# Differential attention: the causal mask added on VectorE with the maximum, instead of by matrix products on TensorE

## The chip, the cores and the metric

The kernel runs on one core of a Trainium2 chip. The core has TensorE for matrix products (PE in the profile; PEld is its loading of weights), VectorE (DVE), ScalarE (ACT), GpSimd (POOL), and SyncE (SP), which here issues DMAs. They work side by side and wait for each other by semaphores. SBUF is the working memory of 128 partitions; PSUM, in eight banks, takes the results of TensorE. The metric is the time of one execution on the device in microseconds (us).

## What is computed

A decoder trunk of two layers over 512 tokens of 1024 numbers. Each layer is a feed-forward block, a token mixer, cross-attention into 256 memory tokens, and another feed-forward block, each followed by a LayerNorm. The mixer of the first layer is differential attention with 8 heads; only it is touched. Cut to what matters:

```python
def diff_attention(x, w_qkv, w_o, lam_q, lam_k, subln_g, cos, sin, lam_init):
    ...
    q = rope(q, c5, s5)
    k = rope(k, c5, s5)
    lam = jnp.exp(jnp.sum(lq[0] * lk[0])) - jnp.exp(jnp.sum(lq[1] * lk[1])) + lam_init
    ...
    def block(args):
        qblk, i = args
        s = jnp.einsum('bqhcd,bkhcd->bhcqk', qblk, k).astype(jnp.float32) * scale
        qpos = i * DA_QBLOCK + jnp.arange(DA_QBLOCK)
        mask = kpos[None, :] <= qpos[:, None]
        s = jnp.where(mask, s, jnp.finfo(jnp.float32).min)
        p = jax.nn.softmax(s, axis=-1)
        a = p[:, :, 0] - lam * p[:, :, 1]
        return jnp.einsum('bhqk,bkhe->bqhe', a.astype(v.dtype), v)
    ...
    o = o * lax.rsqrt(jnp.mean(jnp.square(o), axis=-1, keepdims=True) + LN_EPS)
```

Each head has two score maps (m = 0 and 1), each with its own softmax, and the second is subtracted from the first with a factor. A query sees only keys that do not come after it.

## The kernel before

**Precision.** Every float32 operand of a large product is split into a high part, made by ScalarE, and a low rest, made by VectorE (`split`, lines 114 and 115). A product is then three products: high by high, low by high, high by low (lines 201 to 203). So VectorE and ScalarE must work for each weight before TensorE can use it.

**The stage.** `diff_attention` weaves two streams of work. The main stream (`da_main`) projects values, queries and keys head by head, and at the end multiplies by the first half of the output matrix. After each projection come the rotary step (`da_rope`, lines 941 to 944) and the splits into `qk` and `low` tiles (954 to 970). The side stream (`da_side`) runs over 32 steps, one for each head h and query block i of 128 tokens. In step s it makes the scores of step s (`da_scores`), turns the probabilities of step s - 2 (`da_turn`, four transposes at most, line 479), and multiplies those of step s - 3 with the values (`da_out`, lines 1014 and 1015). After the last block of a head come the norm's factor on GpSimd (1030 to 1033), the scaling on ScalarE (1039) and a last transpose (`da_turn_out`). `weave` gives the side stream a turn for each 900 ns of main work by a fixed table of costs (`W_SC` and others), so where the side stream's work stands among the projections does not hang on what an instruction really takes. Each engine's queue is then put in order when the program is built, and each engine works through its own queue in that order.

**The scores (`da_scores`).** Query block i sees n = 128, 256, 384 or 512 keys. For each map, two products of n columns make the scores in a PSUM bank (lines 983 and 984). A third product, identity by mask in bfloat16, adds a large negative number above the diagonal in the last 128 columns (985). VectorE reduces each row to its negated maximum `mx` (988). ScalarE takes the exponential of PSUM minus the maximum, writes the probabilities `p` to SBUF, and sums each row with a second instruction, the read of its accumulator (both line 989). VectorE then forms the factor from the two sums (992, 993) and subtracts the second map from the first (994). The scores, the transposes and the output products share six PSUM banks in turn (`aux`). There are four `p` tiles; each step takes two.

**Constants.** `da_constants`, beside the first feed-forward block, loads the mask into a temporary tile and casts mask and identity to bfloat16 (1501 to 1504). `NEG`, the number above the diagonal, is minus two to the power of 100.

Of the kernel before, what the change touches and what calls it, by code (L numbers as in the profile page):

```python
# [12 lines left out]
AF = mybir.ActivationFunctionType  # L13
ALU = mybir.AluOpType
AX = mybir.AxisListType
PSUM = bass.MemoryType.PSUM

P = 128
D = 1024
S = 512  # L20
# [13 lines left out]
NEG = -float(2.0**100)  # L34
# [65 lines left out]
def drain(units):  # L100
    for _ in units:
        pass


class Trunk:
# [76 lines left out]
    def mm(self, name):  # L182
        return self.mmp.tile([P, S], F32, tag="mm", name=name)
# [789 lines left out]
    def da_scores(self, st, i):  # L973

        nc = self.nc
        q, k, n = st["q"], st["k"], (i + 1) * P
        qi, kn = slice(i * P, n), slice(0, n)
        mx, rc, cf = self.small("mx"), self.small("rc", (P, 1)), self.small("cf", (P, 1))
        sm = st["sm"][:, i]
        sc = [self.aux("sc")[:, :n] for m in range(2)]  # L980
        mm = nc.tensor.matmul
        for m in range(2):
            mm(sc[m], q[m][:, qi], k[0][m][:, kn], start=True, stop=False)
            mm(sc[m], q[m][:, qi], k[1][m][:, kn], start=False, stop=False)
            mm(sc[m][:, n - P :], self.identr, self.maskr, start=False, stop=True)
        p = [self.tmp("p")[:, :n] for m in range(2)]
        for m in range(2):
            nc.vector.tensor_reduce(mx[:, m : m + 1], sc[m], AX.X, ALU.max, negate=True)
            nc.scalar.activation(
                p[m], sc[m], AF.Exp, bias=mx[:, m : m + 1], accum_out=sm[:, m : m + 1]  # L990
            )
        nc.vector.reciprocal(rc, sm[:, 1:2])
        nc.vector.scalar_tensor_tensor(cf, sm[:, 0:1], self.nlam, rc, ALU.mult, ALU.mult)
        nc.vector.scalar_tensor_tensor(p[0], p[1], cf, p[0], ALU.mult, ALU.add)
        st["p", i] = p[0]
# [73 lines left out]
    def da_side(self):  # L1069

        n = DA_H * NT
        for s in range(n + LS + 2):
            h, i = divmod(s, NT)
            if s < n:
                while h >= len(self.heads) or self.clock < self.heads[h][0] + LEAD:
                    yield WAIT
                self.da_scores(self.heads[h][1], i)
                yield W_SC[i]
            h, i = divmod(s - LT, NT)
            if 0 <= s - LT < n:  # L1080
                self.da_turn(self.heads[h][1], i)
                yield W_T[i]
            h, i = divmod(s - LO, NT)
            if 0 <= s - LO < n:
                while len(self.heads[h][1]["v"]) < NT:
                    yield WAIT
                self.da_out(self.heads[h][1], i)
                yield W_O[i]
            h, i = divmod(s - LS, NT)
            if 0 <= s - LS < n and i == NT - 1:  # L1090
                self.da_scale(self.heads[h][1])
                yield W_E[0]
            h, i = divmod(s - LS - 1, NT)
            if 0 <= s - LS - 1 < n and i == NT - 1:
                self.oT[h] = self.da_turn_out(self.heads[h][1])
                yield W_E[1]
# [370 lines left out]

    def mixer(self, layer, ln):
        if layer == 0:
            bufs = dict(low=4, rt=2, a=4, p=4, o=1, qk=8, _x=0, v=4, oT=11)  # L1470
            with self.other_pools(), self.phase_pool(("v", "v"), "rt", **bufs):
                self.diff_attention(layer, ln)
            self.close_side()
        else:
            w = self.a["xa_wkv"][layer]
            self.later = ExitStack()
            self.later.enter_context(self.late_pools())
            self.kvp = self.later.enter_context(self.pool("kv"))
            with self.phase_pool(("pooled", "pooled"), "sq", pooled=20, sq=1):
                with self.tc.high_priority():  # L1480
                    keys = self.load_cols(w, 0, "rawe")
                    self.load_memory()
                    ahead = [self.halves(t, "we", "we") for t in keys]
                    self.pool_weights()
                    self.raw_order = ["rawe", "raw", "raw"]
                side = self.pool_mixer(layer, ln)
                next(side)
                self.kv = []
                self.weave(self.first_heads(layer, ahead), side, 900, 6000)
                drain(self.early_kv(layer, (1,), self.ahead))  # L1490
            self.close_side()

    def da_constants(self):
        nc, a = self.nc, self.a
        c = lambda shape, name, dt=F32: self.ropep.tile(shape, dt, name=name)
        self.rope = c([P, 2], "rope")
        nc.sync.dma_start(self.rope, a["rope"])
        self.ropeC, self.ropeS = c([P, S], "ropeC"), c([P, S], "ropeS")
        self.rope_tables()
        m = self.tmp("sp", (P, P))  # L1500
        nc.sync.dma_start(m, a["mask"])
        self.maskr, self.identr = (c([P, P], n, mybir.dt.bfloat16) for n in ("maskr", "identr"))
        nc.vector.tensor_copy(self.maskr, m)
        nc.vector.tensor_copy(self.identr, self.ident)
        self.subg = c([P, 1], "subg")
        nc.sync.dma_start(self.subg, a["da_subln_g"].rearrange("a p -> p a"))
        nc.vector.tensor_scalar(self.subg, self.subg, 1.0 - LAM_INIT, None, ALU.mult)
# [29 lines left out]
```

## Time and profile before

| | us |
|---|---|
| median of 3 runs | 1947.85 |
| lowest and highest | 1946.04, 1948.92 |
| the profiled execution | 1946.09 |
| its span, first to last instruction | 1944.3 |
| busy: TensorE, VectorE, ScalarE, GpSimd | 1913.8, 1560.1, 1012.3, 334.3 |

The granted clock of TensorE is 0.998 in the mean. A group of instructions is shown by line, engine, operation, "out<-in" by the program's tile names with the shapes, then busy us and the mean ns of one, then the engine's idle time just before them with what ended it. In the chain of work, each piece is what the following one waited for, or the instruction before it on its engine.

### The profile page before, as it was taken

The numbers are of one execution on the slowest core, as the hardware profiler recorded it, in microseconds if no ns is written. First come the engines' busy times: TensorE is split into PE (matmuls) and PEld (weight loads), VectorE is DVE, ScalarE is ACT, GpSimd is POOL, SyncE is SP. The second block draws the span as 40 slices with busy tenths as digits, with TensorE's granted clock in tenths as the row PEclk, the third lists the DMA queues.
The fourth block names the chain that finished last, engine by engine and source line by source line (L and its number), as shares of the span: only waits on it lengthen the run. The fifth ranks groups of instructions, "written<-read, shape, count | busy, mean of one in ns | idle before, by whom it ended". The sixth has DMA issues, their size and how long they took to land.

```text
span 1944.3 us, 32440 instructions
## 1 busy us (share of the span) xinstructions
PE 1913.8 (98%) x13052; PEld 1741.6 (90%) x13052; DVE 1560.1 (80%) x2200; ACT 1012.3 (52%) x1537; POOL 334.3 (17%) x317
## 2 busy tenths in 40 slices
PE   9999999999999999999999999999999999999998
PEld 8999998888778888999998999999898889999996
DVE  7988987888867557798888888988886468888886
ACT  6555553566655444655554555555455436555552
POOL 3212121111211002312110322122110013111211
PEclk9999999999999999999999999999999999999999
DMA  9878772322135425977695598778445336777861
GB/s 255 198 169 181 169 154 66 90 66 88 44 109 174 128 68 132 226 167 147 153 202 140 105 217 174 169 155 175 142 141 152 109 87 115 192 175 170 183 143 44
DMA packets 254182, 280.58 MB, mean 144 GB/s; under 512 B 9168, under 2 KB 221648, under 8 KB 254032
## 3 DMA queue, kind: packets, MB, share of 16 engines
q0 software_dynamic: 95808, 102.77, 32.4%
q1 hardware_dynamic: 158224, 175.74, 28.2%
q8 instruction: 102, 1.67, 0.3%
q14 instruction: 48, 0.39, 0.1%
HBM read 274.28 MB, written 4.20 MB: 143 GB/s over the span
## 4 chain that ended last, share of the span: by engine, by line
PE 72%; DVE 16%; DMA 4%; ACT 4%; issue 2%; POOL 1%; SPq 0%; DVEq 0%; POOLq 0%; ACTq 0%
PE x L202 6%; PE x L201 6%; PE x L203 6%; PE z L202 4%; PE z L201 4%; PE z L203 4%; DVE wl L115 4%; PE ps L203 3%; PE ps L202 3%; PE ps L201 3%; DMA ra<-in_ffn_w_in_dram 3%; PE px L201 2%; PE px L203 2%; PE px L202 2%; PE xq L202 2%
## 5 line engine op out<-in xcount | busy, mean ns | idle before, releaser
L636 POOL DMA_DIRECT2D ra<-in_ffn_w_in_dram x132 | 170.4, 1313 | 989.1 <-DVE wl L115 968.8
L114 ACT CAST wh<-ra 128x1024 fp32r<-128x1024 f32 x184 | 193.3, 1052 | 212.6 <-PE x L202 59.0
L115 DVE TENSOR_TENSOR wl<-ra,wh 128x1024 fp32r<-128x1024 f32 x184 | 223.7, 1221 | 68.8 <-ACT wh L114 68.0
L114 ACT CAST wh<-rc 128x1024 fp32r<-128x1024 f32 x136 | 142.8, 1053 | 120.7 <-PE x L202 43.6
L201 PE MATMUL x<-xh,wh 128*128 128x256 f32 x704 | 196.8, 280 | 1.3 <-ACT xh L114 1.3
L203 PE MATMUL x<-xh,wl 128*128 128x256 f32 x704 | 196.4, 279 | 0.6 <-DVE wl L115 0.6
L202 PE MATMUL x<-xl,wh 128*128 128x256 f32 x704 | 196.4, 279 | 0.1
L201 PE MATMUL x<-xe,wh 128*128 128x256 f32 x704 | 195.6, 278 | 0.0
L202 PE MATMUL x<-xe,wh 128*128 128x256 f32 x704 | 195.5, 278 | 0.0
L203 PE MATMUL x<-xe,wl 128*128 128x256 f32 x704 | 195.4, 278 | 0.0
L114 ACT CAST wh<-b 128x1024 fp32r<-128x1024 f32 x112 | 117.8, 1051 | 131.0 <-PE x L202 63.2
L115 DVE TENSOR_TENSOR wl<-rc,wh 128x1024 fp32r<-128x1024 f32 x136 | 164.5, 1220 | 22.9 <-ACT wh L114 22.9
L115 DVE TENSOR_TENSOR wl<-b,wh 128x1024 fp32r<-128x1024 f32 x112 | 136.8, 1221 | 41.3 <-ACT wh L114 41.3
L201 PEld LDWEIGHTS x<-xh,wh 128*128 128x128 f32 x704 | 133.1, 189 | 2.8 <-ACT xh L114 1.5
L202 PEld LDWEIGHTS x<-xl,wh 128*128 128x128 f32 x704 | 133.4, 190 | 1.9 <-DVE xl L115 0.6
L203 PEld LDWEIGHTS x<-xh,wl 128*128 128x128 f32 x704 | 133.1, 189 | 0.8 <-DVE wl L115 0.8
L201 PEld LDWEIGHTS x<-xe,wh 128*128 128x128 f32 x704 | 132.6, 188 | 1.3
L202 PEld LDWEIGHTS x<-xe,wh 128*128 128x128 f32 x704 | 132.5, 188 | 1.4
L203 PEld LDWEIGHTS x<-xe,wl 128*128 128x128 f32 x704 | 132.4, 188 | 0.0
L203 PE MATMUL y<-xh,wl 128*128 128x256 f32 x352 | 98.9, 281 | 3.4 <-DVE wl L115 2.3
L201 PE MATMUL y<-xh,wh 128*128 128x256 f32 x352 | 98.2, 279 | 0.4 <-ACT wh L114 0.4
L202 PE MATMUL z<-xe,wh 128*128 128x256 f32 x352 | 97.8, 278 | 0.3 <-DVE xe L115 0.3
(404 smaller groups left out, 6075.8 us busy)
## 6 DMA issues: line engine op xcount, KB each, us to landing
ra<-in_ffn_w_in_dram POOLq DMA_DIRECT2D x132, 512.0 KB, 7.0
rc<-in_ffn_w_in_dram SPq DMA_DIRECT2D x88, 512.0 KB, 6.3
b<-in_ffn_w_out_dram SPq DMA_DIRECT2D x60, 512.0 KB, 5.0
ra<-in_ffn_w_in_dram SPq DMA_DIRECT2D x44, 512.0 KB, 5.0
rc<-in_ffn_w_in_dram POOLq DMA_DIRECT2D x44, 512.0 KB, 7.7
b<-in_ffn_w_out_dram POOLq DMA_DIRECT2D x16, 512.0 KB, 12.4
raw<-in_da_w_qkv_dram SPq DMA_DIRECT2D x16, 512.0 KB, 5.2
raw<-in_xa_wkv_dram SPq DMA_DIRECT2D x8, 1024.0 KB, 5.5
```

The source lines that it names most:

```text
L114: self.nc.scalar.copy(hi, src),
L115: self.nc.vector.tensor_sub(lo, src, hi.bitcast(F32)),
L201: mm(out, w[0], x[0], start=start, stop=False, skip_group_check=again)
L202: mm(out, w[0], x[1], start=False, stop=False, skip_group_check=again)
L203: self.last_mm = mm(out, w[1], x[0], start=False, stop=stop, skip_group_check=again)
L636: self.last_more = nc.gpsimd.dma_start(t, source(*block), accum_op=ALU.add)
```

## The change

The third product of each map goes, and with it the bfloat16 tiles and their casts. In its place stands a float32 tile of 128 by 512: 384 columns of zeros, set by GpSimd, and the mask in the last 128 columns, loaded by SyncE's queue. Taken from column 512 - n on, its n columns are zero but for the last 128. One VectorE instruction, `tensor_tensor_reduce`, adds this to the scores in PSUM, multiplies by -1, writes the n results to the `p` tile in SBUF, and keeps the least of each row, starting from two to the power of 100: that is the negated maximum, as before. The exponential then reads `p` with a factor of -1 and writes `p` in place. The phase's pools get one buffer more (`mask=1`).

```diff
             mm(sc[m], q[m][:, qi], k[0][m][:, kn], start=True, stop=False)
-            mm(sc[m], q[m][:, qi], k[1][m][:, kn], start=False, stop=False)
-            mm(sc[m][:, n - P :], self.identr, self.maskr, start=False, stop=True)
-        p = [self.tmp("p")[:, :n] for m in range(2)]
+            mm(sc[m], q[m][:, qi], k[1][m][:, kn], start=False, stop=True)
+        p, mask = [self.tmp("p")[:, :n] for m in range(2)], self.mask[:, S - n :]
         for m in range(2):
-            nc.vector.tensor_reduce(mx[:, m : m + 1], sc[m], AX.X, ALU.max, negate=True)
+            top = mx[:, m : m + 1]
+            nc.vector.tensor_tensor_reduce(p[m], sc[m], mask, -1.0, -NEG, ALU.add, ALU.min, top)
             nc.scalar.activation(
-                p[m], sc[m], AF.Exp, bias=mx[:, m : m + 1], accum_out=sm[:, m : m + 1]
+                p[m], p[m], AF.Exp, bias=top, scale=-1.0, accum_out=sm[:, m : m + 1]
             )
...
         n = DA_H * NT
+        self.mask = self.tmp("mask")
+        self.nc.gpsimd.memset(self.mask[:, : S - P], 0.0)
+        self.nc.sync.dma_start(self.mask[:, S - P :], self.a["mask"])
         for s in range(n + LS + 2):
...
-            bufs = dict(low=4, rt=2, a=4, p=4, o=1, qk=8, _x=0, v=4, oT=11)
+            bufs = dict(low=4, rt=2, a=4, p=4, o=1, qk=8, _x=0, v=4, oT=11, mask=1)
...
-        m = self.tmp("sp", (P, P))
-        nc.sync.dma_start(m, a["mask"])
-        self.maskr, self.identr = (c([P, P], n, mybir.dt.bfloat16) for n in ("maskr", "identr"))
-        nc.vector.tensor_copy(self.maskr, m)
-        nc.vector.tensor_copy(self.identr, self.ident)
```

## The prediction

> **What bounds the kernel now.** I first read the span in slices (TensorE's granted clock is full throughout), then looked for the stage that the change touches. The masked scores run from about 376 to 576 us, so I asked for the busy time of each engine in four stretches of it. Columns: stretch, its length, then busy us (and count) of PE, PEld, DVE, ACT, POOL, clock, DMA share, GB/s.
>
> ```profile
> 376.00:409.00 33.00, 33.00 (x223) 29.12 (x222) 29.17 (x65) 21.23 (x57) 3.31 (x4) 1.00 0.22 65
> 409.00:455.00 46.00, 46.00 (x294) 39.87 (x293) 39.56 (x84) 31.62 (x83) 8.48 (x12) 1.00 0.25 69
> 455.00:528.00 73.00, 69.27 (x387) 55.44 (x386) 63.10 (x131) 48.99 (x128) 16.67 (x20) 1.00 0.18 58
> 528.00:576.00 48.00, 46.90 (x281) 38.93 (x280) 34.07 (x75) 29.90 (x93) 4.94 (x10) 1.00 0.31 109
> ```
>
> TensorE never idles in the first two stretches, loses 3.7 us in the third and 1.1 us in the fourth. VectorE is 86 to 88% busy in the first three. So TensorE looks like the bound, with VectorE close behind. The chain of work, in order of time, shows how close:
>
> ```profile
> 455.12 0.25 PE q L203
> 455.40 0.74 DVE rt L941 x2
> ...
> 526.61 0.47 ACT p L989 x2
> 527.12 0.66 PE pt L479 x4
> ```
>
> Up to 455 us the chain is TensorE alone; between these two pairs of rows it is nearly all VectorE and ScalarE, for 72 us, and then TensorE again. In that stretch it is the softmax and rotary work that ends last, though TensorE is 95% busy. How far back VectorE had been nearly late is told by its own waits. The first three rows are those from 409.5 to 527 us, the fourth from 528 to 576 us; columns: total us, times, longest.
>
> ```profile
> DVE rc L992 <- ACT p L989: 11.6, 9, 2.7
> DVE rt L941 <- PE k L203: 0.7, 1, 0.7
> DVE rt L941 <- PE q L203: 0.7, 1, 0.7
> ```
> ```profile
> DVE mx L988 <- PE sc L985: 2.4, 3, 1.1
> ```
>
> From 409 to 527 us VectorE waits for TensorE only twice, 1.4 us in all. Its other idle time there is spent on ScalarE: the reciprocal L992 needs the exponentials' sums, and VectorE works in order. After 528 us it again waits for TensorE to produce scores.
>
> **The change part by part.**
>
> *The 64 mask products go.* What one costs is read from the starts of TensorE's instructions around it, not from its shown duration, since products overlap. Columns: start, us, engine, line.
>
> ```profile
> 487.45 0.39 PE L983 MATMUL sc<-qk 128*128 128x512 f32 x1
> 487.68 0.40 PE L984 MATMUL sc<-low,qk 128*128 128x512 f32 x1
> 487.92 0.23 PE L985 MATMUL sc<-maskr,identr 128*128 128x128 bf16 x1
> 487.96 0.48 PE L983 MATMUL sc<-qk 128*128 128x512 f32 x1
> 488.28 0.40 PE L984 MATMUL sc<-low,qk 128*128 128x512 f32 x1
> 488.51 0.23 PE L985 MATMUL sc<-maskr,identr 128*128 128x128 bf16 x1
> 488.56 0.47 PE L201 MATMUL k<-xh,wh 128*128 128x512 f32 x1
> 488.87 0.40 PE L202 MATMUL k<-xl,wh 128*128 128x512 f32 x1
> ```
> ```profile
> 471.40 0.22 PE L983 MATMUL sc<-qk 128*128 128x128 f32 x1
> ...
> 471.76 0.28 PE L984 MATMUL sc<-low,qk 128*128 128x128 f32 x1
> 471.88 0.23 PE L985 MATMUL sc<-maskr,identr 128*128 128x128 bf16 x1
> ...
> 472.23 0.39 PE L202 MATMUL k<-xl,wh 128*128 128x512 f32 x1
> ```
>
> With 512 columns, 1.42 us pass from the first score product to the product after next. Five products of 512 columns at 0.23 us would take 1.16, so two masks cost 0.26, 0.13 each: 0.04 for itself, the rest because the product behind it comes late (0.32 instead of 0.23). With 128 columns the same stretch is 0.83 us; one product at 0.23 and four at 0.12 make 0.71, so 0.06 each. I take 0.13 for the 48 with 256 to 512 columns and 0.06 for the 16 with 128: 7.2 us, a mean of 0.11. The Trainium skill ("TensorE: Matmul & The Clock Gate", section "Back-to-back issue gap") puts a weight load with its product of 128 columns at about 81 ns in a real stream; by that the 64 would be an estimated 5.2 us; the trace's starts say more for the wide ones and less for the narrow. By stretch:
>
> ```profile
> 376.00:409.00 33.00, 3.23 (x14) 1.35 (x14) 1.00 0.22 65
> 409.00:455.00 46.00, 3.23 (x14) 1.36 (x14) 1.00 0.25 69
> 455.00:528.00 73.00, 5.55 (x24) 2.33 (x24) 1.00 0.18 58
> 528.00:576.00 48.00, 2.76 (x12) 1.16 (x12) 1.00 0.31 109
> ```
>
> These are L985 alone (PE, PEld): 14, 14, 24 and 12 products, worth 1.5, 1.5, 2.6 and 1.3 us of TensorE.
>
> *The reduction becomes add, maximum and a write-out.* The combined instruction is in no row of before. The nearest parts are (groups by shape, 376 to 576 us; busy us, mean ns):
>
> ```profile
> L988 DVE TENSOR_REDUCE mx<-sc 128x1 f32<-128x512 f32 x16 | 10.3, 682 | 1.2 <-PE sc L985 1.1
> L988 DVE TENSOR_REDUCE mx<-sc 128x1 f32<-128x128 f32 x16 | 4.0, 279 | 0.0
> L115 DVE TENSOR_TENSOR a<-pt,a 128x512 fp32r<-128x512 f32 x8 | 5.5, 683 | 1.0 <-ACT a L114 1.0
> L115 DVE TENSOR_TENSOR a<-pt,a 128x128 fp32r<-128x128 f32 x8 | 2.3, 284 | 0.1
> L994 DVE SCALAR_TENSOR_TENSOR p<-p,cf 128x512 f32<-128x512 f32 x8 | 6.0, 746 | 0.1
> ```
> ```profile
> L397 DVE DVE_READ_ACCUMULATOR X<-X,ps x64: 79/82/85, 315.1 to 1936.9; 128x1 f32 x64
> ```
>
> A sum of a PSUM tile and an SBUF tile written to SBUF takes what the reduction takes (683 against 682, 284 against 279 ns). An instruction of VectorE that also sums along the row (L397) is followed by a read of the accumulator of 82 ns; I take it that the running minimum is read in the same way. So each of the 64 costs 82 to 87 ns more, 0.084 us, 5.4 us in all. Low end: no such read, 0 more (not below: it passes the same elements and writes more). High end with the same rate: L994's price, 746 + 82 - 682 = 0.15 us. I take 0.084, as the immediates here need no per-row scalar as L994's does.
>
> *The exponential reads SBUF instead of PSUM, in place.* Nearest rows, both of 128 columns with a per-row operand:
>
> ```profile
> L989 ACT ACTIVATE p<-sc,mx 128x128 f32<-128x128 f32 x16 | 5.8, 364 | 4.8 <-DVE mx L988 4.7
> L1039 ACT ACTIVATE o<-o,f 128x128 f32<-128x128 f32 x32 | 11.3, 398 | 14.3 <-POOL f L1033 14.3
> ```
>
> SBUF to SBUF is 34 ns longer, 2.2 us of ScalarE over 64. ScalarE is about two thirds busy, so this counts only where VectorE waits for the sums: two exponentials in each of the 9 waits of L992, 0.6 us.
>
> *The scores' PSUM bank is free when VectorE has read it,* not after the exponential. The transposes at 527.12 waited for an exponential that ended just then; that wait, 0.3 to 0.4 us, goes. What is late next is the lower halves L115 that the products before it need.
>
> *Tiles, memset, DMA.* Two casts and one load in the first feed-forward go, which no later wait hangs on: nothing. The mask's memset is put on POOL, and its load on SP, where the stage's side work begins. Its neighbour on POOL is:
>
> ```profile
> L1103 POOL MEMSET low<- x4: 520/520/522, 312.4 to 314.2; 64x512 f32 x4
> ```
>
> The mask's memset has 384 columns against 512, some 0.4 us; behind it on POOL lie the small steps of the LayerNorm. Behind the load on SP lie query and key weights of the first heads, should its buffer come free late. From these memsets to the scores there are 60 us of projections, which hide both, so I cost them at nothing; exposed, the memset is 0.4 us, and a held weight load a few us. The new tile's writer p waits only for VectorE's own L994 and for transposes three steps back, which TensorE has behind it before it makes the scores.
>
> *The sum.* Up to 409 us TensorE sets the pace: -1.5. From 409 to 527 us VectorE does: 36 larger instructions at 0.084, +3.0; longer exponentials, +0.6; its two waits for TensorE are swallowed, -1.4; the bank, -0.4. TensorE's 4.1 us there turn into waits. After 527 us: -1.3. Sum -1.0 us. The profiled execution took 1946.09 (span 1944.3, 1.8 around it), so 1945.1 against itself; it is 1.8 below the median of the three runs, 1947.85, and against that I say 1946.9.
>
> **The rivals.**
> *Full gain.* TensorE stays in front because its inputs are made several steps ahead and a late VectorE is absorbed; the two uninterrupted stretches speak for it, the 72 us of chain without TensorE against it. All 7.2 us and the bank: 1940.3.
> *VectorE takes over (slower).* If the new instruction costs 0.15 us more and VectorE sets the pace from the first score to 527 us: 50 x 0.15 = 7.5, exponentials 0.8, after 527 us -1.3, bank -0.4: +6.6, 1954.5. It decides once an addition outgrows VectorE's 1.4 us of waits for TensorE over the 36 from 409 us on, 0.04 us each; 0.084 is past this, which is why my sum already loses TensorE's gain there. Against it: chain pieces where VectorE is idle can take in the additions.
> *Half rate.* If the combined instruction passes one element in two cycles: 16 x (128+256+384+512) = 20,480 elements at 1.04 ns (L115's slope, (683-284)/384) are 21 us more; of the 50 before 527 us about 17, to which 4 for the reads come: about +19, 1967. L994 with two SBUF sources isn't slowed so (746 ns, where two cycles for each of 512 elements would be 1,065), and here one source is PSUM. The Trainium skill ("Vector Engine (DVE) Microarchitecture Reference", section "7. Points that are easy to get wrong") says that this shape halves its rate with two SBUF sources that aren't bf16; L994's 746 ns disagree.
> *Order.* All engines' queues are put in order when the program is built, so another set of instructions can shift them: 2 or 3 us either way, within the cases above.
>
> **How the numbers follow.** A difference of 0.2%, 3.9 us, is about what can be told from no change. My sum, with what the order may do (1944 to 1951): 0.46. Full or most of the gain (1940 to 1944): 0.28. VectorE takes over (1952 to 1956): 0.21. Half rate: 0.05. So faster 0.28, within 0.2% 0.46, slower 0.26. The range takes my own case, the full gain and the larger part of the takeover: 1940 to 1954.5.
>
> **What would show it.** After: no L985; the combined instruction at about 765 ns with its read at 512 columns and 366 at 128; exponentials some 34 ns longer; in the stretch that was 409 to 527 us more TensorE idle than 3.7 us, ended by VectorE, and a chain on VectorE that begins earlier than 455 us; the last stretch shorter by 1.3 us. Wrong would be: TensorE's idle not grown (full gain), an instruction over 0.9 us at 512 columns, or a difference that arises outside 376 to 576 us, above all a weight load held up at 345 to 365 us.

## The result and the profile after

| | us |
|---|---|
| after, median of 6 runs | 1941.47 (1938.94 to 1943.77) |
| before, median of 6 runs | 1948.88 (1946.04 to 1950.28) |
| after / before | 0.9963, 95% interval 0.9951 to 0.9976 |
| the profiled execution after, and its span | 1943.24, 1941.4 |
| busy: TensorE, VectorE, ScalarE, GpSimd | 1906.5, 1558.0, 1013.7, 332.8 |

The change makes the kernel 7.4 us faster, 0.37%. The forecast was 1946.9, about no change; 1941.47 lies in the range, but near where the rival "Full gain" put it, at 1940.3.

The first view of after is again the busy time in stretches. Columns: stretch, length, busy us (and count) of PE, PEld, DVE, ACT, POOL, clock, DMA share, GB/s.

```profile
376.00:409.00 33.00, 33.00 (x215) 29.85 (x214) 30.20 (x81) 21.66 (x54) 4.55 (x5) 1.00 0.26 75
409.00:455.00 46.00, 45.67 (x284) 40.40 (x284) 39.31 (x97) 32.28 (x85) 8.51 (x12) 1.00 0.26 70
455.00:528.00 73.00, 69.55 (x388) 59.20 (x387) 66.41 (x164) 51.81 (x136) 17.10 (x20) 0.98 0.17 58
528.00:576.00 48.00, 46.90 (x266) 39.77 (x265) 33.32 (x85) 28.47 (x86) 4.54 (x10) 1.00 0.33 110
```

From 409 to 528 us TensorE idles 0.33 + 3.45 us; before it was 0 + 3.73. The prediction named this as the sign of the full gain: TensorE's idle time has not grown, although 38 products of the mask no longer stand in these two stretches.

How long the scores take from the first to the last is read from one row per kernel: the source line of the first score product, with its count, shortest, median and longest ns, and the us of its first and last start. Before, then after:

```profile
L983 PE MATMUL sc<-qk x64: 218/354/477, 379.3 to 557.3; 128*128 128x128 f32 x16, 128*128 128x256 f32 x16, 128*128 128x384 f32 x16, 128*128 128x512 f32 x16
```
```profile
L983 PE MATMUL sc<-qk x64: 220/334/553, 382.3 to 553.6; 128*128 128x128 f32 x16, 128*128 128x256 f32 x16, 128*128 128x384 f32 x16, 128*128 128x512 f32 x16
```

178.0 us became 171.3. I call this difference the **score span** from here on. It is 6.7 us shorter, and the median is 7.4 us shorter. The profiled execution as a whole is only 2.9 us shorter (1943.24 against 1946.09): it began its scores 3.0 us later, by chance (below), and lost about 1 us behind the stage.

The new instruction and the exponential, in the groups of after by shape (370 to 580 us; busy us, mean ns of one, idle before it):

```profile
L989 ACT ACTIVATE p<-p,mx 128x512 f32<-128x512 f32 x16 | 11.4, 712 | 0.2
L988 DVE CUSTOM_DVE_ANT_0 p<-sc,mask 128x512 f32<-128x512 f32 x16 | 10.5, 684 | 1.1 <-PE sc L984 1.1
...
L989 ACT ACTIVATE p<-p,mx 128x128 f32<-128x128 f32 x16 | 6.3, 397 | 4.6 <-DVE mx L988 4.5
...
L988 DVE DVE_READ_ACCUMULATOR2_ANT mx<- 128x1 f32 x64 | 5.2, 82 | 0.0
...
L988 DVE CUSTOM_DVE_ANT_0 p<-sc,mask 128x128 f32<-128x128 f32 x16 | 4.2, 284 | 0.1
```

The shown durations came out as forecast: 684 and 284 ns with a read of 82 (766 and 366), and 33 ns more for the shortest exponential (397 against 364). But shown durations overlap on VectorE too, as the starts tell. Two reductions of 512 columns before, then two combined instructions after, each pair with what follows it (start, us, engine, line):

```profile
489.68 1.27 DVE L988 TENSOR_REDUCE mx<-sc 128x1 f32<-128x512 f32 x2
490.87 0.69 DVE L942 TENSOR_TENSOR rt<-q,ropeC 128x512 f32<-128x512 f32 x1
```
```profile
490.55 0.68 DVE L988 CUSTOM_DVE_ANT_0 p<-sc,mask 128x512 f32<-128x512 f32 x1
491.14 0.09 DVE L988 DVE_READ_ACCUMULATOR2_ANT mx<- 128x1 f32 x1
491.14 0.69 DVE L988 CUSTOM_DVE_ANT_0 p<-sc,mask 128x512 f32<-128x512 f32 x1
491.75 0.09 DVE L988 DVE_READ_ACCUMULATOR2_ANT mx<- 128x1 f32 x1
491.75 0.69 DVE L942 TENSOR_TENSOR rt<-q,ropeC 128x512 f32<-128x512 f32 x1
```

The read starts some 75 ns before the shown end of its combined instruction, and the next instruction starts with the read. The two reductions hold VectorE for 1.19 us, the two combined instructions for 1.20. Over the stage, where another instruction follows directly, the median step from start to start is 601, 468, 332 and 200 ns for the reduction of 512 to 128 columns, and 611, 478, 343 and 210 for the combined instruction: some 10 ns more, not 84. The time in which line 988 keeps VectorE busy from 370 to 580 us, before and then after, says nearly the same:

```profile
370.00:580.00 210.00, 28.72 (x64) 1.00 0.24 76
```
```profile
370.00:580.00 210.00, 29.61 (x128) 0.99 0.24 76
```

So the change adds 0.6 to 0.9 us to VectorE in the stage, where the prediction counted 5.4. The exponential, from start to start, takes 706 in place of 662 ns at 512 columns, 44 ns more.

### The profile page after: what moved, and what is told of

The parts are those of the page before. It is cut to its first block, busy times and chain, and to the rows that moved or that the text cites. A ratio compares the mean times of both kernels' runs of the same rounds, so it can differ in the third digit from the quotient of the medians.

```text
span 1941.4 us, 32397 instructions
## 1 busy us (share of the span) xinstructions
PE 1906.5 (98%) x12988; PEld 1740.4 (90%) x12988; DVE 1558.0 (80%) x2262; ACT 1013.7 (52%) x1537; POOL 332.8 (17%) x318
## 4 chain that ended last, share of the span: by engine, by line
PE 73%; DVE 15%; DMA 5%; ACT 4%; issue 2%; POOL 1%; SPq 0%; DVEq 0%; POOLq 0%; ACTq 0%
PE x L202 6%; PE x L201 6%; PE x L203 6%; PE z L201 4%; PE z L202 4%; PE z L203 4%; PE ps L203 3%; PE ps L202 3%; PE ps L201 3%; DVE wl L115 3%; DMA ra<-in_ffn_w_in_dram 3%; PE px L201 2%; PE px L203 2%; PE px L202 2%; PE xq L202 2%
```

## The experiments

Two theories stood against each other at first. **"VectorE sets the pace"** is the prediction's: from 409 to 527 us VectorE's additions cost what they take, and TensorE's gain is lost there. **"Full gain"**: the products' 7 us come out whole, whatever is added to VectorE and ScalarE. When the kernels below were built, the additions to VectorE were still taken for 5.4 us. The score spans below are read as in the two rows above, each from one profiled execution; ratios are to the kernel before, run on the same chip.

| kernel | mask products | on VectorE per map | score span, us | median, us | ratio and interval |
|---|---|---|---|---|---|
| before | yes | reduction | 178.0 | 1948.88 | 1 |
| after | no | combined | 171.3 | 1941.47 | 0.9963 (0.9951 to 0.9976) |
| e1_products_only | no | reduction | 171.4 | 1940.79 | 0.9955 (0.9943 to 0.9968) |
| e2_vector_only | yes | combined | 178.5 | 1948.31 | 0.9996 (0.9987 to 1.0004) |
| e3_exp_from_psum | no | combined, bank held | 173.6 | 1945.66 | 0.9979 (0.9969 to 0.9989) |
| e4_constants_kept | no | combined | 170.2 | 1941.09 | 0.9957 (0.9944 to 0.9971) |
| e5_vector_psum | yes | combined, bank held | 177.2 | 1947.72 | 1.0000 (0.9991 to 1.0009) |
| e6_more_vector | no | combined (copies elsewhere) | 170.2 | 1938.59 | 0.9958 (0.9946 to 0.9971) |
| e7_products_more_vector | no | reduction (copies elsewhere) | 171.3 | 1942.90 | 0.9975 (0.9964 to 0.9985) |
| e8_join_later | no | combined | 177.9 | 1949.74 | 1.0009 (1.0000 to 1.0018) |
| e9_one_chained | no | combined + 1 copy | 180.1 | 1951.21 | 1.0013 (1.0004 to 1.0022) |
| e10_three_chained | no | combined + 3 copies | 184.7 | 1954.52 | 1.0032 (1.0019 to 1.0044) |
| e11_scale_later | no | combined | 175.0 | 1945.37 | 0.9983 (0.9974 to 0.9992) |
| e12_half_chained | no | combined + 1 copy on one map | 175.8 | 1947.29 | 1.0000 (0.9991 to 1.0008) |

### One part of the change at a time

**e1_products_only**: the kernel before, with line 985 gone (and `stop=True` on 984) and the rest as it was. The causal mask is left out.

> The kernel before without the 64 mask products, and nothing else changed: reduction, exponential from PSUM and constants stay. The causal mask is left out. 'Absorbed' (VectorE's additions fit into the lead that the buffers give, so TensorE's 7.2 us come in full): 7 us faster than before, 1942, and the stretch from 409 to 527 us shorter by 4, as in the changed kernel. 'Bank' (VectorE does set the pace from 409 to 527 us, and the scores' banks freed before the exponential pay for it): without the early bank only the ends of the stage gain, 3 to 4 us faster, 1945. The forecast's own sum (VectorE sets the pace, nothing pays): 4 us faster.

**e2_vector_only**: the changed kernel with the mask products and their constants kept; the mask is then added twice.

```diff
-            mm(sc[m], q[m][:, qi], k[1][m][:, kn], start=False, stop=True)
+            mm(sc[m], q[m][:, qi], k[1][m][:, kn], start=False, stop=False)
+            mm(sc[m][:, n - P :], self.identr, self.maskr, start=False, stop=True)
```

> The changed kernel with the mask products and their constants kept, so that the mask is added twice: VectorE and ScalarE as in the changed kernel, TensorE as before. 'Absorbed': the same as before within 1 us, 1949. 'Bank': 3 us faster than before, 1946, since the early bank is worth more than the 0.084 us for each reduction. The forecast's own sum: 2 to 3 us slower than before, 1951.5.

Without the products and with VectorE's instructions as before, the whole gain is there: 0.9955, a score span of 171.4 us. If VectorE had set the pace from 409 to 527 us in the kernel before, e1 could have gained no more than the 2.8 us outside it and VectorE's 1.4 us of waits for TensorE in it. And the combined instruction alone costs nothing that shows: 0.9996, 178.5 against 178.0 us. Since it adds under 1 us, e2 does not tell what a larger addition would cost. After is e1 plus the combined instruction, and its score span is that of e1. In both kernels TensorE's order is that of before but for the products; some of VectorE's and ScalarE's instructions stand at other places in their queues.

### The bank, and the constants

**e3_exp_from_psum**: the changed kernel, with the exponential reading the scores in PSUM as before, so that the bank is held until it has ended. The mask is left out of the probabilities.

```diff
-                p[m], p[m], AF.Exp, bias=top, scale=-1.0, accum_out=sm[:, m : m + 1]
+                p[m], sc[m], AF.Exp, bias=top, accum_out=sm[:, m : m + 1]
```

> The changed kernel with the exponential reading the scores in PSUM again, so that a bank is held until the exponential is done. The mask then counts in the maximum alone and is left out of the probabilities. 'Absorbed': as the changed kernel within 1 us, 1941.5 (ScalarE 2 us less busy). 'Bank': 3 to 4 us slower than the changed kernel, 1945.

**e4_constants_kept**: the changed kernel, with the removed load and casts of the constants put back beside the first feed-forward, unused.

> The changed kernel with the mask's load and both casts kept beside the first feed-forward block, unused. The profile of the changed kernel has 3.0 us of waits of TensorE for VectorE at 63 to 69 us that the one before lacks, behind a weight split that stands one place later in VectorE's queue. If that order comes from the three instructions taken out: 2 to 3 us faster than the changed kernel, 1939. If it is chance of one execution: the same, 1941.5.

**e5_vector_psum**: e2 with e3's edit, so that products, combined instruction and held bank stand together.

> The mask products stay, the reduction is the combined instruction, and the exponential reads the scores in PSUM, so the bank is held until it has ended, as before. Mask and probabilities are complete (the mask enters the maximum twice). Against e2_vector_only, which differs only in where the exponential reads. Theory 'Bank' (the early release of the score banks is worth about 4 us, and pays for VectorE's 5.4 us and ScalarE's longer exponentials): about 1952, 3 to 5 us over e2, and in the stage from 376 to 528 us waits of TensorE's score products and of its transposes on ScalarE's exponentials, as e3 had them. Theory 'Chance of order' (what e3_exp_from_psum lost came from one late exponential and the lower clock behind it, not from the bank as such): as e2 or the kernel before, 1947 to 1949.

e4 is the changed kernel again (0.9957): the casts cost nothing. e3 lost 2.3 us of score span against after, and about 3 us by the ratios. Two waits of TensorE that after does not have are in it (us in total, times, longest; 376 to 530 us):

```profile
PE sc L983 <- DVE cf L993: 2.9, 1, 2.9
...
PE pt L479 <- ACT p L989: 1.2, 1, 1.2
```

Taken whole, that would make the early release of the bank worth 2 to 3 us, not 0.3 to 0.4; but only the second of these waits, 1.2 us, ended with an exponential. And e5 holds the bank as well and loses nothing against e2 (1.0000 against 0.9996; 177.2 against 178.5 us). So the bank's worth stays open: it may count only where TensorE is as far ahead as without the products, or e3's loss may come from its queue order on VectorE and ScalarE, which is not the same as that of after.

### More work on VectorE

How much more can VectorE take? **e6_more_vector** and **e7_products_more_vector** were to answer this with one more VectorE instruction behind each combined one (e6) and behind each reduction of e1 (e7):

```diff
             nc.vector.tensor_tensor_reduce(p[m], sc[m], mask, -1.0, -NEG, ALU.add, ALU.min, top)
+            nc.vector.tensor_copy(self.small("more", (P, 1)), self.nlam)
```

> The changed kernel with one more VectorE instruction behind each combined one, a copy of one column that nobody reads: 64 of about 0.13 to 0.16 us, 8 to 10 us of VectorE in the stage, 6 of them from 409 to 527 us. Theory 'VectorE sets the pace from 409 to 527 us' (the prediction's): the time rises by what is added there, about 6 us, to 1947. Theory 'Absorbed' (the inputs of the score products are made steps ahead, and VectorE's idle time takes the addition): 0 to 2 us more than the changed kernel, 1941 to 1943.

> e1_products_only (the kernel before without its mask products; the causal mask is left out) with the same extra VectorE copy behind each reduction: VectorE carries as much as in the changed kernel or somewhat more, the exponentials read PSUM and cost what they cost before, and the bank is held until they end. Theory 'Bank' (a later exponential holds the bank and so stops TensorE): about 1945, 3 to 5 us over e1. Theory 'Absorbed': within 1.5 us of e1, 1940.5 to 1942.5; then what e3_exp_from_psum lost needs another cause than VectorE's load with a held bank.

They missed their aim. The copies need nothing of the stage, and when the queues were put in order they were moved ahead of it. The source line of the copies in e6, with its first and last start:

```profile
L989 DVE COPY more<-nlam x64: 139/142/147, 357.0 to 364.1; 128x1 f32<-128x1 f32 x64
```

They ran beside the LayerNorm. What is left of them is useful all the same: in the stage, all engines of e6, and of e4, have the queue order of after, and all those of e7 have that of e1. So e4 and e6 repeat after (0.9957 and 0.9958 against 0.9963), and e7 repeats e1 (0.9975 against 0.9955, with score spans of 171.3 and 171.4). Two kernels with the same stage can thus differ by 0.2% in the ratio, 3.9 us, and by 1.1 us in the score span. By the ratio, the losses of e3 and of e11 (below) are not clear of this.

**e9_one_chained, e10_three_chained, e12_half_chained** hold the copy in its place: it copies the maximum onto itself, and the exponential needs it. e9 has one for each map, e10 three, e12 one for the second map alone.

```diff
-            nc.vector.tensor_tensor_reduce(p[m], sc[m], mask, -1.0, -NEG, ALU.add, ALU.min, top)
+            nc.vector.tensor_tensor_reduce(p[m], sc[m], mask, -1.0, -NEG, ALU.add, ALU.min, top); nc.vector.tensor_copy(top, top)
```

> The changed kernel with one VectorE copy of the maximum onto itself between each combined instruction and its exponential. The exponential needs its result, so it can't be moved to another stage, as the 64 copies of e6_more_vector were (they ran from 357 to 364 us). Each copy takes about 0.14 us (e6's row): 64 are 9 us of VectorE, and the 36 from 409 to 527 us 5.1. Theory 'VectorE sets the pace from 409 to 527 us': about 5 us over the changed kernel, 1946 to 1947 beside a kernel before of 1948. Theory 'Absorbed' (VectorE's waits for the exponentials' sums, 8.8 us of its idle there, shrink by what is added): 0 to 2 us over it, 1941 to 1943.

> As e9_one_chained with three such copies: 27 us more of VectorE in the stage, 15.3 of them from 409 to 527 us, where the changed kernel's VectorE idles 12.5 us. Theory 'VectorE sets the pace': about 15 us over the changed kernel, 1956. Theory 'Absorbed': what the idle time can't take in is lost, and more, since not all of the idle time lies at the right place: 5 to 12 us over it, 1946 to 1953. If even this costs under 3 us, VectorE is far from setting the pace there.

> The changed kernel with the chained copy of e9_one_chained behind the second map's combined instruction alone: 32 copies of 0.15 us, 4.8 us of VectorE in the stage, 2.6 of them from 409 to 527 us. VectorE then carries 10 us more than with the reduction; the change itself adds 5.4 (and cost 0 to 1 us), e9 14.9 (and cost 10). Theory 'Slack' (VectorE has room for some 5 us more in the stage, and what goes past it costs TensorE waits and a lower clock behind each): about 1945 to 1947 beside a kernel before of 1948.8, half of e9's loss. Theory 'Edge' (the changed kernel stands at the edge already): near e9, 1949 to 1951. Theory 'Room for 10 us': as the changed kernel, 1941 to 1943.

Here an addition costs at last. The copies of e9, by source line:

```profile
L988 DVE COPY mx<-mx x64: 133/149/155, 385.3 to 563.7; 128x1 f32<-128x1 f32 x64
```

By the ratios e12 loses 7 us against after, e9 10 and e10 13; by the score span 4.5, 8.8 and 13.4. e9 lost more than either of its theories gave, e12 lies between "Slack" and "Edge", and e10 between its two. Shown durations would make the copies 4.8, 9.5 and 28 us of VectorE, but they overlap with their neighbours here as well. From e9:

```profile
501.71 0.29 DVE L988 CUSTOM_DVE_ANT_0 p<-sc,mask 128x128 f32<-128x128 f32 x1
501.93 0.08 DVE L988 DVE_READ_ACCUMULATOR2_ANT mx<- 128x1 f32 x1
501.93 0.15 DVE L988 COPY mx<-mx 128x1 f32<-128x1 f32 x1
501.99 0.55 DVE L115 TENSOR_TENSOR a<-pt,a 128x384 fp32r<-128x384 f32 x1
502.46 0.14 DVE L988 COPY mx<-mx 128x1 f32<-128x1 f32 x1
```

The next instruction starts some 0.07 us behind a copy, so that e12's 32 copies hold VectorE for some 2.2 us and e9's 64 for some 4.5. What they delay is more: one copy here stands behind the other map's combined instruction, the other behind a split. From the shown end of a combined instruction to the start of its exponential 0.60 us pass in the mean in after; in the second map of e12 it is 1.10 us, in e9 1.20, in e10 2.27. The score span itself, in after, e12 and e9, shows what TensorE lost:

```profile
382.30:553.60 171.30, 167.53 (x1010) 147.03 (x1009) 149.52 (x389) 119.27 (x322) 29.66 (x40) 0.99 0.22 68
```
```profile
381.50:557.30 175.80, 168.26 (x1011) 145.95 (x1010) 152.22 (x420) 120.73 (x323) 28.75 (x40) 1.00 0.22 67
```
```profile
381.50:561.60 180.10, 170.59 (x1010) 149.34 (x1009) 153.39 (x451) 121.03 (x323) 30.77 (x40) 0.97 0.21 65
```

TensorE idles for 3.8, 7.5 and 9.5 us, and its clock is at half for 3.4, 0 and 10.2 us. So of the 4.3 us between e12 and e9 the larger part goes with the lower clock behind longer waits (last section), and what more copies cost does not follow their number. In e9 TensorE now waits long for the maximum (376 to 590 us):

```profile
PE sc L983 <- DVE mx L988: 4.9, 2, 4.3
PE sc L983 <- DVE a L115: 3.6, 2, 2.6
```

So the change's own addition, under 1 us, was free, and 32 small copies ahead of the exponential took back most of the gain, or all of it by the ratio. It was not that VectorE had no idle time left. Its own waits in e12, 409 to 528 us:

```profile
DVE rc L992 <- ACT p L989: 12.5, 9, 2.4
```

That wait was 8.8 us in after (below), and it grew. The copy delays the exponential, the exponential delays the sums, and VectorE, working in order, waits for them with the rotations and splits behind it. One limit stays: each of these kernels has an order of its own on VectorE and ScalarE, so the amount added, its place ahead of the exponential and the order were not separated. How much work VectorE could take at a place where nothing waits for it was not measured.

### Two attempts to go further

**e8_join_later**: reciprocal, factor and subtraction (992 to 994) moved to a function of their own, called one step later in the side stream, with `p=6`.

```diff
+        st["join", i] = p, rc, cf, sm
+
+    def da_join(self, st, i):
+        nc = self.nc
+        p, rc, cf, sm = st.pop(("join", i))
         nc.vector.reciprocal(rc, sm[:, 1:2])
...
                 self.da_scores(self.heads[h][1], i)
-                yield W_SC[i]
+            h, i = divmod(s - 1, NT)
+            if 0 <= s - 1 < n:
+                self.da_join(self.heads[h][1], i)
+            if s < n:
+                yield W_SC[s % NT]
```

> The changed kernel with the reciprocal, the factor and the subtraction of a step issued one step later, and six probability buffers in place of four. It takes away VectorE's waits for the exponentials' sums (10.6 us in 12 waits from 376 to 528 us). Theory: these waits delay the rotations and the subtractions that TensorE's remaining waits in the stage stand on (3.6 us for VectorE's a from 376 to 528 us, and the lower clock behind the longest): the stage gets 1 to 3 us shorter, 1938.5 to 1940.5. Rival: VectorE's waits sit beside work that nobody needs at once, and the subtraction a step later makes the transposes wait: 1941 to 1944.

**e11_scale_later**: the scaling of a head's output a step later.

```diff
-LT, LO, LS = 2, 3, 4
+LT, LO, LS = 2, 3, 5
...
-            bufs = dict(low=4, rt=2, a=4, p=4, o=1, qk=8, _x=0, v=4, oT=11, mask=1)
+            bufs = dict(low=4, rt=2, a=4, p=4, o=2, qk=8, _x=0, v=4, oT=11, mask=1)
```

> The changed kernel with the scaling of a head's output (and the transpose behind it) one step later, and two output tiles in place of one. It takes away ScalarE's waits for GpSimd's factor (7.9 us in 5 waits from 410.8 to 524 us), which stand ahead of the splits of queries and keys in ScalarE's queue. Theory: the last 3 us of TensorE's waits in the stage hang on these splits, and 1 to 3 us of them go: 1938.5 to 1940.5 beside a kernel before of 1948. Rival, as e8_join_later came out: the wait moves to another place of the same ring of ScalarE, VectorE and GpSimd: no gain, or a loss of some us.

Both lost. e8 did cut the wait it was made to cut, from 8.8 to 3.9 us, but another took its place (VectorE, 410.6 to 530 us):

```profile
DVE a L115 <- ACT a L114: 6.1, 5, 1.8
DVE rc L997 <- ACT p L989: 3.9, 4, 2.6
```

In after the first of these was 1.3 us. TensorE's waits for low parts, 3.6 us in after from 376 to 528 us with a longest of 2.5, are now, from 410.6 to 530 us,

```profile
PE sc L983 <- DVE a L115: 7.5, 4, 4.5
```

and the score span is 177.9 us. In e11 it is 175.0. By the ratio e8 lost 9 us against after, more than its rival gave, and e11 4. No kernel here beats the changed one by more than repeats differ.

## Why the prediction was right in its range and wrong in its sum

The range held because it had been drawn to take in the full gain too, which had a chance of 0.28. The sum itself forecast a gain of 1.0 us where 7.4 came.

*The shown durations were right.* The combined instruction, its read and the longer exponential came out within 2 ns. Half rate is excluded.

*The products' price was right.* Setting the starts of the same TensorE instructions in both traces against each other (medians over some ten each), after gains on before 1.5 us from the start of the scores to 409 us (forecast 1.5), and 1.5 after 528 us (1.3). e1 puts the whole at 6.6 us of score span, against 7.2 counted.

*The step that failed* is in the sum: "From 409 to 527 us VectorE does [set the pace]: 36 larger instructions at 0.084, +3.0", with "TensorE's 4.1 us there turn into waits". I forecast +1.8 us there; there the same instructions come 3.8 us closer together. Two things in it are wrong.

The first is the size of the term. I had read TensorE's products from their starts, since their durations overlap, and then added VectorE's read by its duration. From start to start the 36 cost some 10 ns each, 0.4 us, not 3.0. By the prediction's own rule, that VectorE decides once each addition is past 0.04 us, TensorE's gain there was then not to be lost.

The second is the pace itself. In e1 nothing is added to VectorE, and the same instructions come 4.2 us closer together. VectorE did not hold TensorE back there, even without an addition. With 0.4 for 3.0 the sum would still be -3.6 us; the rest of the 6.7 us lies in TensorE's 4.1 us that I had turned into waits. The evidence I took for this was the chain of waits, nearly all VectorE and ScalarE from 455 to 527 us. In after this chain even begins earlier, as I had said it would:

```profile
410.48 0.24 PE q L203
410.75 0.76 DVE rt L941 x2
...
522.47 0.48 DVE a L115
523.00 0.39 PE sc L983
```

It now leads for 112 us in place of 72, and TensorE lost nothing. The chain tells what happened to end last in that execution; it does not tell that VectorE had no slack. The slack was in VectorE's own idle time, which I had listed and then taken as fixed. Between the same TensorE instructions (to 0.3 us), before and after:

```profile
409.50:527.00 117.50, 113.88 (x669) 94.21 (x668) 101.51 (x212) 79.11 (x207) 25.15 (x32) 1.00 0.21 63
```
```profile
410.80:524.80 114.00, 110.23 (x633) 94.90 (x632) 101.52 (x248) 80.28 (x205) 25.61 (x32) 0.99 0.21 65
```

The second has 36 products of TensorE fewer, those of the mask, and 36 instructions of VectorE more, the reads of the accumulator. VectorE is busy for 101.5 us in both, since the reads lie within the time of their neighbours; and its idle time falls from 16.0 to 12.5 us. In e1, where nothing was added, it falls to 13.0 us (busy 100.47 of 113.5 us). Its waits in that stretch of after:

```profile
DVE rc L992 <- ACT p L989: 8.8, 9, 2.6
DVE a L115 <- ACT a L114: 1.3, 2, 0.8
DVE qk L955 <- ACT qk L954: 0.3, 1, 0.3
```

The waits for the exponentials' sums went from 11.6 to 8.8 us, and the 1.4 us of waits for TensorE went altogether. The latter I had taken off; the former I had kept whole. In e1, where VectorE had nothing added, they are 8.4 us. So a faster TensorE goes with shorter waits of VectorE for ScalarE. Two causes are open: the exponentials hang on TensorE's scores and come earlier; and with other instructions the queues of VectorE and ScalarE are put in order anew. They were not tried apart. TensorE's own order is the same in before, e1, e2 and after but for the products.

*The rival "VectorE takes over"* has the right kind of mechanism and the wrong point. I put the point at 0.04 us for each instruction. The change's addition, 0.010, is under it, so the change never put this rival to the test. e12, with copies that take some 0.035 in the mean, has no gain left by the ratio, but there the exponential is held up too.

*The bank* was put at 0.3 to 0.4 us. e3 points at 1 to 3, e5 at nothing; it stays open.

*Memset, load and constants at nothing*: e4 confirms the constants; no weight load of after was seen held up. The scores of after's profiled execution started 3.0 us later than before's, but those of e6, with the same stage, at 379.3 like before's. About half of it arose ahead of the LayerNorm, the rest there, from the clock, as the last section shows.

## What to carry to other kernels

Price an instruction by the starts of it and of its successor, on every engine. Here a read of 82 ns behind a VectorE instruction cost 10. A chain of waits on another engine is not a bound on the engine that you relieve: ask of each idle stretch of that engine what ends it, and whether it shrinks when the relieved engine runs ahead. The cheapest test is to take away the one part alone (e1), then to add the other alone (e2). To test for the edge, a free addition does not do, since it is moved elsewhere when the queues are ordered; one that is chained into the work stays, but it also delays what waits for it: 32 chained copies, some 2.2 us of VectorE, lost by the ratio all that this change had gained.

## What the runs showed of the hardware

TensorE's clock falls after waits that are short beside the stage. In after, TensorE's row at 500.82 us follows a wait of 2.46 us (start, us, engine, line):

```profile
497.74 0.39 PE L203 MATMUL q<-xh,wl 128*128 128x512 f32 x1
...
500.82 0.55 PE L983 MATMUL sc<-qk 128*128 128x256 f32 x1 [2.46 <-DVE a L115]
...
501.39 0.63 PE L201 MATMUL q<-xh,wh 128*128 128x512 f32 x1
501.81 0.63 PE L202 MATMUL q<-xl,wh 128*128 128x512 f32 x1
...
504.66 0.39 PE L202 MATMUL q<-xl,wh 128*128 128x512 f32 x1
504.89 0.40 PE L203 MATMUL q<-xh,wl 128*128 128x512 f32 x1
```

Behind it products start 0.42 us apart in place of 0.23, and at 504.66 they are back at 0.23; the granted clock from 500 to 505 us is 0.66. So for some 3.5 us TensorE went at about half its rate, which cost 1.7 us there beside the wait's own 2.5. A wait of 1.35 us at the same place of before had no such end, nor had e12, whose longest was 1.1.

The length of the wait alone does not decide. Inside each execution the stretches at half clock are 3.41 us long (once 6.83), and they start a whole number of such lengths apart, as if on a fixed grid: in after at 357.25 and 500.61 us, 143.36 apart, which is 42 times 3.413. e1 and e7 have the same order and the same wait of 2.36 us, but it lies otherwise on the grid. Two successive windows of e1's grid, then of e7's, are

```profile
494.49:497.90 3.41, 1.05 (x6) 0.75 (x6) 2.70 (x10) 2.89 (x8) 0.90 (x1) 1.00 0.07 25
497.90:501.31 3.41, 3.41 (x11) 2.73 (x12) 3.41 (x7) 1.60 (x7) 0.39 (x1) 0.50 0.02 5
```
```profile
493.41:496.82 3.41, 1.93 (x12) 1.46 (x10) 2.67 (x9) 2.39 (x7) 0.00 (x0) 1.00 0.39 152
496.82:500.24 3.42, 2.54 (x14) 2.19 (x15) 3.42 (x8) 1.65 (x6) 1.29 (x1) 1.00 0.02 5
```

In e1 the whole wait lies in one window, and the next is at half clock; in e7 it is spread over two, 1.48 and 0.88 us, and the clock stays full. In all 14 executions here, from 20 to 1900 us, a window with 1.97 us or more of idle TensorE was followed by half clock, none with under 1.40 was, and between 1.40 and 1.85 both occurred. The two score spans are still the same, 171.4 and 171.3 us: beside e7, the same instructions come 1.6 us later in e1 at 510 us, and 0.1 at 527. So such a loss may be taken back.

The same holds for the gap at the LayerNorm, where TensorE is busy for about 10 of 12 us in both kernels; before, then after:

```profile
352.00:364.00 12.00, 10.17 (x67) 8.77 (x66) 7.90 (x14) 5.10 (x9) 0.00 (x0) 1.00 0.34 105
```
```profile
352.00:364.00 12.00, 10.02 (x64) 8.98 (x63) 6.77 (x14) 5.16 (x10) 0.00 (x0) 0.86 0.29 93
```

In before this idle time falls into two windows, 1.00 and 0.98 us; in after 1.76 us of it fall into one.

The Trainium skill ("TensorE: Matmul & The Clock Gate", section "Part 1: The HAM clock gate (the "warmup" mystery)") says that the clock halves after an idle window of about 3.4 us that runs on without regard to the program, and is full again after about as long a busy one. The difference between e1 and e7, and the return some 3.5 us after the restart, agree; that an idle time of 1.40 to 2.46 us in such a window is enough does not.
